# SiLU of convolved channels as one ScalarE function, GpSimd's first-phase work on VectorE, and another order of blocks, banks and priorities in a hybrid decoder layer

## The chip, the cores and the metric

The kernel runs on one core of one Trainium2 chip. A core has five engines that run their own instruction streams in order and wait for one another by semaphores: TensorE (PE, with its weight loads shown apart as PEld), VectorE (DVE), ScalarE (ACT), GpSimd (POOL) and SyncE (SP), which here only issues DMAs. The metric is the device time of one execution in microseconds (us). Before the change the median of three runs is 1030.03 us (1029.24 to 1030.16).

## What is computed

One decoder layer with 16 learned meta tokens ahead of 512 tokens, model width 2048, all float32:

```python
h = rms_norm(concat([meta, x]), norm_w)
(dq, dk, dv, dz, db, da, gq, gk, gv, gz, gl, fq, fk, fv, fz, ff) = split_cols(h @ w_in)
# A: gated DeltaNet, 6 heads x 128
qkv = silu(causal_depthwise_conv(concat([dq, dk, dv], -1), conv_w))
q_dn, k_dn = l2_normalize(q) * 128 ** -0.5, l2_normalize(k)
o_dn = gated_head_norm(gated_delta_rule_chunked(q_dn, k_dn, v_dn, log_a, beta), dz, dn_norm_w)
# B: GLA linear attention, 5 heads (dk 64, dv 128)
o_gla = gated_head_norm(gla_chunked(gq * 64 ** -0.5, gk, gv, log_g), gz, gla_norm_w)
# C: forgetting attention, 5 heads x 128
o_fox = forgetting_attention(fq * 128 ** -0.5, fk, fv, log_f) * silu(fz)
out = rms_norm(x + concat([o_dn, o_gla, o_fox], -1) @ w_out, final_norm_w)
```

`gated_head_norm(o, z, w)` is an RMS norm of each head times `w` and times `silu(z)`. So a SiLU stands in two kinds of place: over the convolved channels dq, dk, dv (18 blocks of 128 channels), and over the gates dz (6 blocks), gz and fz (5 blocks each).

## The kernel before

**The planner.** The kernel is written as many small generators ("chains") that yield operations, events and requests for buffers. A planner, `Weave`, holds an estimate of when each engine is free and when each buffer region is ready (`cost`, `ready`, `emit`), and in `run` always emits the operation with the lowest key: estimated start plus the chain's priority (a lower number goes first), for TensorE plus `SLACK` = 0.25 us. A matmul chain of small ("light") operations is put behind a heavy one when too much light work has come in a row. What it emits is the program order of each engine; so the order is fixed when the kernel is built, and an instruction that is late on the chip holds up all that stands behind it on its engine. All engine calls go through line 251, which is why the profile shows L251 nearly everywhere; tiles, not lines, tell operations apart. `Slots` are pools of buffers: `row` (4 tiles of 128x528), `wide` (9 of 128x1056), `bank` (the 8 PSUM banks), `raw`, `hi`, `lo` (weights as loaded, and split). `Get` waits for a free slot, and where it has `keep`, for more than so many.

**Number format.** A float32 operand is split into a high and a low part (`hp`, `lp` for the pairs, `hb..`, `lb..` for the fill blocks, `ho`, `lo` for the output weights): ScalarE casts the high part, VectorE or GpSimd subtracts it from the operand. A product is three matmuls: high x high, high x low, low x high. `GP = (2,)` sends the subtraction of the second operand of every pair to GpSimd; of the output weights every other one goes there.

**First phase (to 488 us).** Four blocks dz and the gate columns, two more dz (`Z45`), then 18 pairs of 128-column blocks (`PAIRS`, `mm_pair`), each pair as seven half-size products (a Strassen-like scheme; `sums` forms the operands on VectorE, `evac_pair` takes the partial results out of PSUM on ScalarE and VectorE). The pairs alternate between two convolved blocks (dk first, then dv, then dq) and two others (gk, gv, fk, fv). `store` then multiplies the block by the tokens' `rstd` on GpSimd and, for a convolved block, runs `conv`: the first tap on ScalarE, three taps on VectorE, then the SiLU in five steps: a lower bound on GpSimd, Exp, Ln (with bias 1) and Exp on ScalarE, the product on VectorE. `token_rows` transposes the result on TensorE into a bank (`pkdk`, `pkdv`, `pkdq`), takes sums of squares and scaled copies out of it on ScalarE and stores the rows in DRAM. `silu_row` does the same five steps for the gates z (`st..` is its scratch row).

Beside the pairs run `gates` (decay and gate columns, priority 1.0; it sets `e_gate`, for which every `token_rows` waits), `key_scales` (factors of all six key heads at once, as soon as the sums of squares of all six are there; it then starts the next two), `an_blocks` (ten blocks of decay-weighted key products, priority 0.2) and `inverse` (30 steps of two VectorE operations each on tile `ab`, scratch `ot`, which invert 32x32 diagonal blocks).

**Later phases (488 to 1028 us).** The 17 fill blocks (`FILL`: gq, fq, gz, fz in this order) are plain products of 48 matmuls of 512 columns each; they stand in TensorE's order between the mixers' small matmuls. `phase_b` starts when all pairs have left and the inverse is stored: DeltaNet (`dn_group`, `levels`, `core` with its recurrence over blocks, `tail`). `phase_c` runs GLA and the forgetting attention side by side, `phase_d` starts when all fill blocks are done: the output projection (`po`, last column `pz`), the residual, and the final norm (`norm_out`: Ln and Exp on ScalarE for `frs`). Line 345 loads one table set for ScalarE by name:

```python
nc.scalar.preload_act_table_set("natural_log_exp_and_others")
```

The small matmuls that the prediction names: `pm` (DeltaNet's triangular inverse, from `an`), `pks` (the recurrence, from `y`, the result on its way through ScalarE), `pgo` (GLA's output, from `gon`), `pss` (GLA's scores), `pfa`, `pfw` (forgetting attention), `ptl` (the gates' last product, from `scm`).

Of the kernel before, what the change touches and what calls it, by code (L numbers as in the profile page):

```python
# [13 lines left out]
AF = mybir.ActivationFunctionType  # L14
# [59 lines left out]
NBLK = len(COLS) // P  # L74
NROW, NMS, NPB, NWG, NWF, NTS, NOP = 4, 16, 6, 19, 24, 9, 17
GPRI, FPRI = 0.0, 0.0
GP, KX = (2,), 5
AP, KA, BACK, XP = 0.2, 2, 3.0, 0.6
LIGHT, SLACK, DMAL = 0.8, 0.25, 0.8
# [5 lines left out]
class Op:  # L85
    __slots__ = ("eng", "call", "a", "kw", "outs", "ins", "dur", "lat", "dma", "light")

# [55 lines left out]
class Engine:  # L143
# [3 lines left out]
    def __getattr__(self, what):  # L147
        real, key = getattr(self.real, what), self.key

        def make(*a, **kw):  # L150
            op = Op()
            op.eng, op.call, op.a, op.kw = key, real, a, kw
            aps = [x for x in a if isinstance(x, bass.AP)]
            outs = []
            if "out" in kw:
                outs.append(kw["out"])
            elif aps:
                outs.append(aps.pop(0))
# [8 lines left out]
            op.dur, op.lat, op.dma = cost(key, what, n, outs[0], ins)  # L167
            op.light = key == "P" and (n < 64 or ins[0].shape[0] < P or ins[0].free_size() < P)
            return op

        return make
# [38 lines left out]
class Weave:  # L210

    def __init__(self, tc):
        self.tc, self.t, self.last, self.state, self.chains = tc, {}, {}, {}, []
        self.base, self.n, self.light = 0.0, 0, 0.0

# [19 lines left out]
    def emit(self, op):  # L235
        start = max(self.t.get(op.eng, 0.0), self.ready(op))
        if op.eng == "P":
            idle = start - self.t.get("P", 0.0)
            self.light = self.light + idle + op.dur if op.light else max(0.0, self.light + idle - op.dur)
        end = done = start + op.dur  # L240
        self.t[op.eng] = end
        if op.dma:
            self.t["D"] = max(self.t.get("D", 0.0), end + 1.5) + op.dma
            done = self.t["D"] + DMAL
        else:
            done += op.lat
# [4 lines left out]
        i = op.call(*op.a, **op.kw)  # L251
# [7 lines left out]
    def go(self, gen, pri=0.0, name=""):  # L259
        self.n += 1  # L260
        c = [gen, pri, self.n, None, 0.0, name or getattr(gen, "__name__", "")]
        self.chains.append(c)
        self.step(c, None)
# [56 lines left out]
def tile_hybrid_trunk(ctx, tc, xT, xtok, mtok, w_gate, w_in, w_out, consts, lmask, fin_w, out, dbg=None):  # L320
# [19 lines left out]
    tp_s = slots("tp").add(tp, 16, "tp", (P, 2, T))  # L340
    wide_s = slots("wide").add(pa, 9, "pa", (P, 2, T))
    bank_s = slots("bank").add(psp, 8, "k", (P, 512))
# [257 lines left out]

    def key_scales():
        yield tuple(e_nk.values()) + (e_gate,)
        yield A.activation(nbt, gcol[:, :, 0:6], AF.Exp)
        yield A.activation(nbg, gcol[:, :, 6:12], AF.Exp)
        yield A.activation(br, nks, AF.Ln, bias=eps_c)
        yield A.activation(br, br, AF.Exp, scale=-0.5)
        yield V.tensor_tensor(out=nbt, in0=nbt, in1=br, op=ALU.mult)
        yield V.scalar_tensor_tensor(out=nb2, in0=nbt, scalar=-1.0, in1=br, op0=ALU.mult, op1=ALU.mult)
        yield V.tensor_copy(br, nbt)
        yield V.tensor_tensor(out=nbg, in0=nbg, in1=nb2, op=ALU.mult)  # L610
        e_keys.set()
# [7 lines left out]
    e_nk, e_nq, e_keys, e_lq = evs(*range(DN_HEADS)), evs(*range(DN_HEADS)), Ev(), Ev()  # L619
    kds, vps = ([drp.tile([P, NN, P], F32, name=f"{n}{g}") for g in range(2)] for n in ("kds", "vps"))  # L620
# [64 lines left out]
    def token_rows(key, c, u):  # L685
        what, h = key
        g, j = divmod(h, H)
        blocks = [slice(b * P, (b + 1) * P) for b in range(NB)]
        dst, dstm, scale, acc_, ev = {"dk": (kds, kms, dl, nks, e_gate), "dv": (vps, vms, br, None, e_keys),
                                      "dq": (None, None, None, nqs, e_gate)}[what]  # L690
# [78 lines left out]
    def evac_pair(p):  # L769
# [17 lines left out]
        bank_s.give(z)  # L787
        W.go(store(p, 0, u[0]), 0.3, f"store{i}0")
        yield p.done[7]
# [4 lines left out]
        bank_s.give(x)  # L794
        W.go(store(p, 1, u[1]), 0.3, f"store{i}1")
        yield (sp_of(p.keys[0]), sp_of(p.keys[1]))
# [34 lines left out]

    class Block:
# [39 lines left out]
    def operands(seq):  # L872
        yield e_feed
        for it, n in seq:
# [109 lines left out]
    e_A, e_dn, e_fill, e_c, e_gla, e_fox = Ev(), Ev(), Ev(), Ev(), Ev(), Ev()  # L984
    big_s, m_s, pb_s, keep_s = (slots(n) for n in ("big", "m", "pb", "keep"))

    def phase_b():
        yield tuple(p.left for p in pairs) + (e_gate, e_inv)
        early.close()
        W.base = max(W.t.values())  # L990
        kp, bp, mp, pp = pool("kp"), pool("bp", mid), pool("mp", mid), pool("pp", mid)
# [3 lines left out]
        pb_s.add(pp, NPB, "pb", (P, T))  # L995
        for t in range(2):
# [17 lines left out]
    def dn_group(g):  # L1014
# [759 lines left out]
    W.go(loads(), 0.0, "loads")  # L1774
    W.go(key_scales(), 0.1, "scales")
    W.go(mm_main(), 0.25, "mm")
# [67 lines left out]
```

## Time and profile before

| | |
|---|---|
| runs, median (lowest to highest) | 1030.03 us (1029.24 to 1030.16) |
| the profiled execution, its own time | 1029.72 us |
| its span, first to last instruction | 1027.8 us |
| mean granted TensorE clock | 0.985 of full |
| DMA | 144.05 MB, mean 140 GB/s |

The profile shows one execution. For each engine a table of busy time stands first, then 40 equal slices of the span with the busy share of each engine in tenths and the granted clock of TensorE. Groups of instructions are named `out<-in` by the program's tiles with their count, busy time, mean, and the idle time of the engine ahead of them with what ended it. A wait `PE pm <- DMA an<-ans` says that TensorE sat idle ahead of a matmul into `pm` and that the end of that DMA released it. A table of windows gives the same busy times for chosen stretches of the span; restricted to a tile it counts only instructions that read or write it. The slices of TensorE and its clock:

```profile
PE   8999999999999899999998999999999899999996
...
PEclk8999999999999999999998999999999999999998
```

### The profile page before, as it was taken

How to read it: one execution, taken by the hardware profiler on the slowest of the kernel's cores; microseconds unless marked ns; L12 is line 12 of the kernel's file. 1: busy time of each engine (PE TensorE's matmuls, PEld its weight loads, DVE VectorE, ACT ScalarE, POOL GpSimd, SP SyncE). 2: the span in 40 equal slices, each digit the busy share in tenths (PEclk: the TensorE clock that was granted, in tenths of full speed). 3: DMA queues.
4: the chain of work that ended last, by engine and by line, in shares of the span. 5: the costliest groups of instructions: out<-in, count | busy, mean ns of one | idle time of the engine just before them, and what ended most of it. 6: DMA issues, size and time to landing. Idle time of an engine off the chain costs nothing. (4 is left out here: it accounts for less than half of the span.)

```text
span 1027.8 us, 18890 instructions
## 1 busy us (share of the span) xinstructions
PE 983.9 (96%) x7339; PEld 853.3 (83%) x7339; DVE 722.4 (70%) x1178; ACT 535.8 (52%) x1179; POOL 275.3 (27%) x204
## 2 busy tenths in 40 slices
PE   8999999999999899999998999999999899999996
PEld 6889999989999899998776897666767677788885
DVE  6878999778999898888573365857577666633334
ACT  6675555438575675655323574656556543412335
POOL 0022442323344344335101131111131221112451
PEclk8999999999999999999998999999999999999998
DMA  9833222334334354444449526332313444522334
GB/s 325 311 131 124 95 105 74 135 113 153 132 130 152 102 173 146 155 143 117 129 138 318 170 70 217 103 117 84 114 62 104 158 146 148 170 87 82 103 103 163
DMA packets 78060, 144.05 MB, mean 140 GB/s; under 512 B 14461, under 2 KB 38525, under 8 KB 77972
## 3 DMA queue, kind: packets, MB, share of 16 engines
q1 hardware_dynamic: 77972, 142.86, 42.0%
q8 instruction: 57, 0.93, 0.4%
q14 instruction: 31, 0.25, 0.1%
HBM read 119.22 MB, written 23.61 MB: 139 GB/s over the span
## 5 line engine op out<-in xcount | busy, mean ns | idle before, releaser
L251 ACT CAST hp<-a 128x1024 fp32r<-128x1024 f32 x90 | 94.2, 1050 | 60.6 <-PE px L251 35.3
L251 PE MATMUL px<-xh,hp 128*128 128x264 f32 x432 | 125.0, 289 | 0.0
L251 PE MATMUL px<-xh,lp 128*128 128x264 f32 x432 | 123.4, 286 | 1.0 <-DVE lp L251 1.0
L251 PE MATMUL px<-xl,hp 128*128 128x264 f32 x432 | 123.7, 286 | 0.0
L251 DVE SCALAR_TENSOR_TENSOR lp<-a,hp 128x1024 fp32r<-128x1024 f32 x72 | 94.6, 1316 | 20.1 <-ACT hp L251 19.1
L251 POOL TENSOR_TENSOR u<-u,rstd 128x528 f32<-128x528 f32 x36 | 60.1, 1671 | 144.5 <-DVE u L251 109.6
L251 PE MATMUL po<-ho,oh 128*128 128x512 f32 x232 | 93.9, 405 | 1.4 <-ACT oh L251 1.4
L251 PE MATMUL po<-ho,ol 128*128 128x512 f32 x232 | 92.5, 399 | 1.7 <-DVE ol L251 1.7
L251 PE MATMUL po<-lo,oh 128*128 128x512 f32 x232 | 92.1, 397 | 0.0
L251 PE MATMUL px<-tbh,hp 128*128 128x264 f32 x288 | 83.1, 289 | 0.0
L251 PEld LDWEIGHTS px<-xh,lp 128*128 128x128 f32 x432 | 82.0, 190 | 1.2 <-DVE lp L251 1.2
L251 PE MATMUL px<-tbh,lp 128*128 128x264 f32 x288 | 82.3, 286 | 0.5 <-DVE lp L251 0.4
L251 PE MATMUL px<-tah,hp 128*128 128x264 f32 x288 | 82.2, 285 | 0.0
L251 PEld LDWEIGHTS px<-xh,hp 128*128 128x128 f32 x432 | 81.9, 190 | 0.1
L251 PEld LDWEIGHTS px<-xl,hp 128*128 128x128 f32 x432 | 82.0, 190 | 0.0
L251 PE MATMUL px<-tal,hp 128*128 128x264 f32 x288 | 81.9, 284 | 0.0
L251 PE MATMUL px<-tah,lp 128*128 128x264 f32 x288 | 81.8, 284 | 0.0
L251 PE MATMUL px<-tbl,hp 128*128 128x264 f32 x288 | 81.8, 284 | 0.0
L251 ACT CAST ho<-o 128x1024 fp32r<-128x1024 f32 (+1 forms) x35 | 33.9, 976 | 77.2 <-PE po L251 43.6
L251 DVE TENSOR_TENSOR acc<-acc,po 128x512 f32<-128x512 f32 x44 | 29.3, 685 | 53.5 <-PE po L251 53.4
L251 POOL TENSOR_TENSOR lo<-o,ho 128x1024 fp32r<-128x1024 f32 x14 | 33.5, 2396 | 118.5 <-ACT ho L251 100.2
L251 DVE SCALAR_TENSOR_TENSOR cv<-u,cpk,cv 128x525 f32<-128x525 f32 (+2 forms) x54 | 59.5, 1104 | 5.1 <-ACT cv L251 4.2
(375 smaller groups left out, 2748.8 us busy)
## 6 DMA issues: line engine op xcount, KB each, us to landing
a<-in_w_in SPq DMA_DIRECT2D x72, 512.0 KB
o<-in_w_out SPq DMA_DIRECT2D x32, 512.0 KB
rfq<-in_w_in SPq DMA_DIRECT2D x10, 512.0 KB
rgz<-in_w_in SPq DMA_DIRECT2D x10, 512.0 KB
rfz<-in_w_in SPq DMA_DIRECT2D x10, 512.0 KB
fraw<-in_w_in SPq DMA_DIRECT2D x16, 256.0 KB
xt<-in_xtok SPq DMA_DIRECT2D x8, 512.0 KB
acc<-in_xtok SPq DMA_DIRECT2D x16, 256.0 KB
```

Source lines behind the costliest of these rows:

```text
L251: i = op.call(*op.a, **op.kw)
```

## The change

1. **SiLU.** In `conv` the five steps become one ScalarE activation with the function Silu, in place. In `silu_row` the same is done for dz; gz and fz keep the five steps, with the lower bound on VectorE.
2. **GpSimd's work to VectorE.** The product with `rstd` in `store`, the subtractions of operand 2 of the pairs (`GP = ()`), and those of the output weights.
3. **Planner.** It adds 1.3 us where a Silu follows an Exp or Ln on ScalarE or the reverse. A chain can have its own slack for TensorE: 3.0 us for the token rows, 2.0 for the `an` blocks, 1.0 for `levels`. The main matmul chain is served first when slots come free.
4. **Order.** `gates` from priority 1.0 to 0.1, stores from 0.3 to 0.0, `an_blocks` from 0.2 to -0.2. `key_scales` runs once for each group of three heads and starts its own `an` blocks; the scales of the queries and `inverse` (0.05) become chains of their own. The fill blocks go in the order `FORD`.
5. **Buffers.** Two `row` tiles in place of four and ten `wide` in place of nine in the first phase; two more `row` tiles from `phase_b` on; an unused pool is gone.

```diff
-NROW, NMS, NPB, NWG, NWF, NTS, NOP = 4, 16, 6, 19, 24, 9, 17
+NROW, NWIDE, NMS, NWG, NWF, NTS, NOP = 2, 10, 16, 19, 24, 9, 17
-GP, KX = (2,), 5
-AP, KA, BACK, XP = 0.2, 2, 3.0, 0.6
+FORD = 'gq0 fq0 gq1 fq1 fz0 gz0 gz1 fq2 fz1 fq3 fz2 gz2 gz3 fq4 fz3 fz4 gz4'
+STP, IP = 0.0, 0.05
+GP, KX = (), 5
+AP, KA, BACK, XP, GAP = -0.2, 2, 3.0, 0.6, 0.1
...
+            op.fn = {AF.Exp: "e", AF.Ln: "e", AF.Silu: "s"}.get(fn) if key == "A" else None
...
+        if op.fn and op.fn != self.fn:
+            self.fn = op.fn
+            end = done = end + 1.3
...
-            for c in sorted(self.chains, key=lambda c: (c[1], c[2])):
+            for c in sorted(self.chains, key=lambda c: (c[5] != "mm", c[1], c[2])):
...
-                    k = max(c[4] + (SLACK if e == "P" else 0.0), self.t.get(e, 0.0),
+                    k = max(c[4] + (c[6] if e == "P" else 0.0), self.t.get(e, 0.0),
...
     def silu_row(z, key, dst):
+        if key[0] == "dz":
+            yield A.activation(z, z, AF.Silu)
+            yield SP.dma_start(out=dst, in_=z)
+            return
         t = yield Get(row_s, f"st{key[0]}{key[1]}")
-        yield G.tensor_scalar_max(t[:, :S], z, LOW)
+        yield V.tensor_scalar_max(t[:, :S], z, LOW)
...
-    def key_scales():
-        yield tuple(e_nk.values()) + (e_gate,)
...
-        for g in range(2):
-            W.go(an_blocks(g), AP + 0.02 * g, f"an{g}")
-        W.go(inverse(), AP, "inverse")
+    def key_scales(g):
+        c = slice(H * g, H * g + H)
+        yield tuple(e_nk[h] for h in range(c.start, c.stop)) + (e_gate,)
...
+        e_keys[g].set()
+        W.go(an_blocks(g), AP, f"an{g}", 2.0)
...
-        W.go(store(p, 0, u[0]), 0.3, f"store{i}0")
+        W.go(store(p, 0, u[0]), STP, f"store{i}0")
...
     def store(p, n, u):
-        yield G.tensor_tensor(out=u, in0=u, in1=rstd, op=ALU.mult)
+        yield VT(out=u, in0=u, in1=rstd, op=ALU.mult)
...
-            W.go(token_rows(key, c, u), -0.1, f"rows{key[0]}{key[1]}")
+            W.go(token_rows(key, c, u), -0.1, f"rows{key[0]}{key[1]}", 3.0)
...
-        yield G.tensor_scalar_max(t, c, LOW)
-        yield A.activation(t, t, AF.Exp, scale=-1.0)
-        yield A.activation(t, t, AF.Ln, bias=1.0)
-        yield A.activation(t, t, AF.Exp, scale=-1.0)
-        yield VT(out=c, in0=c, in1=t, op=ALU.mult)
+        yield A.activation(c, c, AF.Silu)
...
-    FILL = [Block(("gq", p)) for p in range(2)] + [Block(("fq", h)) for h in range(FOX_HEADS)] \
-        + [Block(("gz", h)) for h in range(GLA_HEADS)] + [Block(("fz", h)) for h in range(FOX_HEADS)]
+    FILL = [Block((k[:2], int(k[2]))) for k in FORD.split()]
...
-                yield from operand(it.src, it.op, it.name, False, True, GT if it.kp % 2 else VT)
+                yield from operand(it.src, it.op, it.name, False, True, VT)
...
+        row_s.add(kp, 4 - NROW, "row_", (P, T))
...
-        W.go(levels(g), -0.2, f"levels{g}")
+        W.go(levels(g), -0.2, f"levels{g}", 1.0)
...
-    W.go(gates(), 1.0, "gates")
+    W.go(gates(), GAP, "gates")
...
-    W.go(key_scales(), 0.1, "scales")
+    for g in range(2):
+        W.go(key_scales(g), 0.1, f"scales{g}")
+    W.go(query_scales(), 0.1, "qscales")
+    W.go(inverse(), IP, "inverse")
```

More of the change, by code (lines that the diff above doesn't have):

```diff
@@ L85 @@
 class Op:
-    __slots__ = ("eng", "call", "a", "kw", "outs", "ins", "dur", "lat", "dma", "light")
+    __slots__ = ("eng", "call", "a", "kw", "outs", "ins", "dur", "lat", "dma", "light", "fn")
 class Ev:
@@ L167, in make @@
             op.dur, op.lat, op.dma = cost(key, what, n, outs[0], ins)
+            fn = next((x for x in a + tuple(kw.values()) if isinstance(x, mybir.ActivationFunctionType)), None)
+            op.fn = {AF.Exp: "e", AF.Ln: "e", AF.Silu: "s"}.get(fn) if key == "A" else None
             op.light = key == "P" and (n < 64 or ins[0].shape[0] < P or ins[0].free_size() < P)
@@ L213, in __init__ @@
         self.tc, self.t, self.last, self.state, self.chains = tc, {}, {}, {}, []
-        self.base, self.n, self.light = 0.0, 0, 0.0
+        self.base, self.n, self.light, self.fn = 0.0, 0, 0.0, "e"
     def begin(self, t, base):
@@ L257, in emit, with go @@
         return start
-    def go(self, gen, pri=0.0, name=""):
+    def go(self, gen, pri=0.0, name="", slack=None):
         self.n += 1
-        c = [gen, pri, self.n, None, 0.0, name or getattr(gen, "__name__", "")]
+        c = [gen, pri, self.n, None, 0.0, name or getattr(gen, "__name__", ""), SLACK if slack is None else slack]
         self.chains.append(c)
@@ L340, in tile_hybrid_trunk @@
     tp_s = slots("tp").add(tp, 16, "tp", (P, 2, T))
-    wide_s = slots("wide").add(pa, 9, "pa", (P, 2, T))
+    wide_s = slots("wide").add(pa, NWIDE, "pa", (P, 2, T))
     bank_s = slots("bank").add(psp, 8, "k", (P, 512))
@@ L599, in gates, with query_scales @@
         e_gate.set()
-    def key_scales():
-        yield tuple(e_nk.values()) + (e_gate,)
[L603 to L611, printed above, removed]
-        for g in range(2):
-            W.go(an_blocks(g), AP + 0.02 * g, f"an{g}")
-        W.go(inverse(), AP, "inverse")
+    def key_scales(g):
+        c = slice(H * g, H * g + H)
+        yield tuple(e_nk[h] for h in range(c.start, c.stop)) + (e_gate,)
+        t, n2, r, ng = (a[:, :, c] for a in (nbt, nb2, br, nbg))
+        yield A.activation(t, gcol[:, :, c], AF.Exp)
+        yield A.activation(ng, gcol[:, :, 6 + c.start : 6 + c.stop], AF.Exp)
+        yield A.activation(r, nks[:, :, c], AF.Ln, bias=eps_c)
+        yield A.activation(r, r, AF.Exp, scale=-0.5)
+        yield V.tensor_tensor(out=t, in0=t, in1=r, op=ALU.mult)
+        yield V.scalar_tensor_tensor(out=n2, in0=t, scalar=-1.0, in1=r, op0=ALU.mult, op1=ALU.mult)
+        yield V.tensor_copy(r, t)
+        yield V.tensor_tensor(out=ng, in0=ng, in1=n2, op=ALU.mult)
+        e_keys[g].set()
+        W.go(an_blocks(g), AP, f"an{g}", 2.0)
+    def query_scales():
         yield tuple(e_nq.values())
@@ L617, in key_scales @@
         e_lq.set()
-    e_nk, e_nq, e_keys, e_lq = evs(*range(DN_HEADS)), evs(*range(DN_HEADS)), Ev(), Ev()
+    e_nk, e_nq, e_keys, e_lq = evs(*range(DN_HEADS)), evs(*range(DN_HEADS)), evs(0, 1), Ev()
     kds, vps = ([drp.tile([P, NN, P], F32, name=f"{n}{g}") for g in range(2)] for n in ("kds", "vps"))
@@ L688, in token_rows @@
         blocks = [slice(b * P, (b + 1) * P) for b in range(NB)]
-        dst, dstm, scale, acc_, ev = {"dk": (kds, kms, dl, nks, e_gate), "dv": (vps, vms, br, None, e_keys),
+        dst, dstm, scale, acc_, ev = {"dk": (kds, kms, dl, nks, e_gate), "dv": (vps, vms, br, None, e_keys[g]),
                                       "dq": (None, None, None, nqs, e_gate)}[what]
@@ L794, in evac_pair @@
         bank_s.give(x)
-        W.go(store(p, 1, u[1]), 0.3, f"store{i}1")
+        W.go(store(p, 1, u[1]), STP, f"store{i}1")
         yield (sp_of(p.keys[0]), sp_of(p.keys[1]))
@@ L984, in tile_hybrid_trunk @@
     e_A, e_dn, e_fill, e_c, e_gla, e_fox = Ev(), Ev(), Ev(), Ev(), Ev(), Ev()
-    big_s, m_s, pb_s, keep_s = (slots(n) for n in ("big", "m", "pb", "keep"))
+    big_s, m_s, keep_s = (slots(n) for n in ("big", "m", "keep"))
     def phase_b():
@@ L990, in phase_b @@
         W.base = max(W.t.values())
-        kp, bp, mp, pp = pool("kp"), pool("bp", mid), pool("mp", mid), pool("pp", mid)
+        kp, bp, mp = pool("kp"), pool("bp", mid), pool("mp", mid)
         keep_s.add(kp, 2, "kp", (P, NN, P))
@@ L994, in phase_b @@
         m_s.add(mp, NMS, "m", (P, H, P))
-        pb_s.add(pp, NPB, "pb", (P, T))
+        row_s.add(kp, 4 - NROW, "row_", (P, T))
         for t in range(2):
```

## The prediction

> **What bounds the kernel now.** The page first, then the table of windows, cut where the TensorE (PE) changes its work: 87.4 to 488.5 us holds the 18 projection pairs (the first phase), 488.5 to 1018.9 the fill blocks, the three mixers and the output projection. Columns: busy us and instructions of PE, its weight loads, VectorE (DVE), ScalarE (ACT), GpSimd (POOL), then granted PE clock, DMA share, GB/s.
>
> ```profile
> PE 983.9 (96%) x7339; PEld 853.3 (83%) x7339; DVE 722.4 (70%) x1178; ACT 535.8 (52%) x1179; POOL 275.3 (27%) x204
> ```
>
> ```profile
> 87.40:488.50 401.10, 387.32 (x3148) 382.49 (x3147) 352.22 (x355) 234.70 (x465) 150.56 (x82) 1.00 0.39 128
> 488.50:1018.90 530.40, 513.38 (x3810) 402.54 (x3809) 301.01 (x712) 240.19 (x617) 111.73 (x101) 0.99 0.40 131
> 204.00:222.00 18.00, 15.86 (x117) 15.36 (x116) 13.35 (x19) 5.87 (x8) 5.58 (x3) 0.91 0.27 94
> 542.00:556.00 14.00, 10.42 (x170) 7.78 (x171) 4.20 (x10) 4.87 (x9) 0.88 (x2) 0.76 1.04 360
> 817.40:845.00 27.60, 23.25 (x94) 18.41 (x94) 19.40 (x29) 14.33 (x27) 8.66 (x7) 0.88 0.43 141
> ```
>
> PE is busy in 387.32 of 401.10 us and in 513.38 of 530.40. The change neither adds nor removes a matmul, so it can only take PE's idle time and the clock lost behind it: 13.8 + 17.0 us idle, and in the last three windows busy time at less than full clock, 15.86 x 0.09 = 1.4, 10.42 x 0.24 = 2.5 and 23.25 x 0.12 = 2.8 us. Next the table of waits for PE alone, by phase (us in total, times, longest):
>
> ```profile
> PE pkdv L251 <- DVE cv L251: 5.4, 4, 1.8
> PE pkdq L251 <- DVE cv L251: 2.8, 2, 2.2
> PE pkdk L251 <- DVE cv L251: 2.2, 1, 2.2
> PE px L251 <- DVE lp L251: 1.3, 2, 1.0
> PE ptl L251 <- DVE scm L251: 1.2, 1, 1.2
> ```
>
> ```profile
> PE pm L251 <- DMA an<-ans: 3.6, 1, 3.6
> PE po L251 <- DVE ol L251: 1.7, 1, 1.7
> PE pfa L251 <- DVE fp L251: 1.7, 2, 1.4
> PE pss L251 <- DVE qx L251: 1.7, 1, 1.7
> PE po L251 <- ACT oh L251: 1.4, 1, 1.4
> PE pfw L251 <- DVE ml L251: 1.3, 2, 1.2
> PE pkdq L251 <- DVE cv L251: 1.1, 1, 1.1
> ```
>
> The greatest cause is one chain: the token rows (`pkdk`, `pkdv`, `pkdq`) are transposed on PE straight after the SiLU of a convolved channel, and PE reaches them before it is done: 5.4 + 2.8 + 2.2 + 1.1 = 11.5 us. The rest is small and scattered.
>
> **The change, part by part.**
>
> *SiLU and GpSimd's work.* By tile (ns min/median/max):
>
> ```profile
> L251 POOL TENSOR_TENSOR u<-u,rstd x36: 1314/1482/2292, 103.0 to 505.0; 128x528 f32<-128x528 f32 x36
> L251 POOL TENSOR_SCALAR u<-cv x18: 1525/2165/2707, 110.4 to 485.4; 128x528 f32<-128x528 f32 x18
> ```
>
> ```profile
> L251 ACT ACTIVATE u<-u x54: 626/644/649, 114.0 to 491.7; 128x528 f32<-128x528 f32 x54
> ```
>
> ```profile
> L251 DVE SCALAR_TENSOR_TENSOR cv<-u,cpk,cv x54: 752/768/2966, 105.7 to 484.2; 128x525 f32<-128x525 f32 x18, 128x526 f32<-128x526 f32 x18, 128x527 f32<-128x527 f32 x18
> L251 DVE SCALAR_TENSOR_TENSOR cv<-cv,u x18: 691/698/2896, 118.9 to 493.3; 128x528 f32<-128x528 f32 x18
> ```
>
> ```profile
> L251 DVE SCALAR_TENSOR_TENSOR lp<-a,hp x72: 1206/1222/2285, 77.7 to 491.9; 128x1024 fp32r<-128x1024 f32 x72
> ```
>
> A convolved channel loses GpSimd's maximum (2.165), two of three activations (2 x 0.644) and VectorE's product (0.698): the chain ahead of the transposes is 4.2 us shorter. The table set that line 345 loads is named for Exp and Ln; whether a Silu needs another no row shows, and I assume that it does. The one load in the trace:
>
> ```profile
> 0.73 1.28 ACT L345 ACT_TABLE_LOAD   x1 [0.73 <-PEq L1836]
> ```
>
> So 2.9 us are left even where each Silu pays a load, against a longest wait of 2.2; and the planner now sets the transposes 3.0 us after it thinks them ready, and costs the load at 1.3. I take 10.5 of the 11.5 us, between 0 and 11.5. How long a Silu takes no row shows; between 0.6 (`u<-u`) and three of those, I take one. The six gate blocks z of the DeltaNet get the same cut; PE waits for none of them. Two `row` tiles for four hold them back more; the ends are 0 and 3 us (the row of the longest wait but one, 2.2, rounded up), and I take 0, since PE has its pairs to do meanwhile and takes banks first.
>
> VectorE takes over 36 products with `rstd`, 18 operand subtractions (`lp` of operand 2) and, later, 14 `lo` and ten maxima. It is at 352.22 of 401.10 us already, so this decides. But the maxima of the rows above are far over their minima, on VectorE, where GpSimd works beside it. The same window for the instructions on `cv`, then on `a`, shows the total:
>
> ```profile
> 87.40:488.50 401.10, 13.66 (x80) 8.50 (x80) 77.17 (x71) 19.40 (x42) 36.80 (x18) 1.00 0.39 128
> ```
>
> ```profile
> 87.40:488.50 401.10, 195.75 (x141) 91.09 (x87) 44.50 (x17) 1.00 0.39 128
> ```
>
> The first has 54 steps and 17 products: at their minima 54 x 0.752 + 17 x 0.691 = 52.4, so 24.8 of 77.17 us are stretch. The second (columns DVE, ACT, POOL) has 141 instructions of one size: 141 x 1.206 = 170.0, stretch 25.7. GpSimd's 150.56 us go but for the masks of the `an` blocks, under 9 us,
>
> ```profile
> L251 POOL TENSOR_SCALAR_AFFINE_SELECT an<-an 128x384 f32<-128x384 f32 x8 | 7.5, 935 | 21.9 <-DMA an<-gd 21.4 <-PE px L251 0.5
> ```
>
> and I let the stretch go with them: 352.2 - 50.5 - 11.7 (products) + 35 x 0.691 + 17 x 1.206 = 334.7. The inverse, which moves into this phase, adds:
>
> ```profile
> 488.50:545.00 56.50, 20.92 (x60) 1.00 0.48 142
> ```
>
> That makes 356 of 401: no new bound, and `lp` half as long as GpSimd's. Cost 0; if the stretch stayed, 414 (below).
>
> *Order of gates, key scales, inverse.* With priority 0.1 for 1.0 the gates run earlier, when their inputs are there; the waits for `scm` and `lp` (1.2, and 1.0 of the 1.3) and their clock (1.4) stand in the window 204 to 222. I take 2.5 of 3.6; a wait may come back elsewhere, so the ends are -1 and 3.6. Key scales by group and priority -0.2 start the ten `an` blocks and the inverse earlier, their DMAs on SP's queue with them (five issues for each `an` block, ten for the inverse), ahead of weight loads; the raw weights have buffers, and VectorE's, not GpSimd's, results are what SP then waits for. The phase after it starts with its inputs in DRAM, and one of PE's longest waits, `pm` on `an<-ans` (3.6, and 2.5 of clock), has more fill blocks to stand behind: I take 4, between 0 and 6.1. Four more short activations and four more short products of the split scales are 2 us on engines with room.
>
> *Order of the fill blocks, banks to matmuls first, stores earlier.* The handover at 817 (3.1 of waits, 2.8 of clock) keeps its chain (cast, subtraction, matmul); only its subtraction loses GpSimd beside it: 1, between -3 and 5.9. Of `pfa`, `pss`, `pfw` (4.7) I take 1, between -4 and 4.7: a new order makes waits of its own.
>
> **Gain: 10.5 + 2.5 + 4 + 1 + 1 = 19 us.**
>
> *What the Silu does to Exp and Ln.* The kernel names one table set for both, by hand, once, at the start; the trace has that one load. The diff names it nowhere again. If a load after a Silu is placed for the function that is next, Exp and Ln may not share a set from then on, and every Ln among Exps costs two loads. Of Lns after the last Silu there are, by row and by code:
>
> ```profile
> L251 ACT ACTIVATE f<-f,eps_c x8: 281/297/313, 587.0 to 621.8; 128x3 f32<-128x3 f32 x8
> ```
>
> ```profile
> L251 ACT ACTIVATE gso<-gso,eps_c x5: 297/297/298, 689.4 to 789.8; 128x4 f32<-128x4 f32 x5
> ```
>
> ```profile
> L251 ACT ACTIVATE frs<-frs,eps_c x4: 294/294/295, 1008.7 to 1020.7; 128x1 f32<-128x1 f32 x4
> ```
>
> and ten in the SiLU of the other gate blocks, three in the GLA gates: 30, so up to 60 loads x 1.28 = 77 us, which the planner doesn't know of. ScalarE is busy in 240.19 of 530.40 us, 45%; a load in its idle time costs nothing, so some 27 delay something. How much of that PE has in hand differs:
>
> ```profile
> 586.63 0.48 ACT L251 COPY y<-pks 128x384 f32<-128x384 f32 x1 [0.56 <-PE pks L251]
> ```
>
> ```profile
> 587.16 0.94 PE L251 MATMUL pks<-y,kd 128*128 128x128 f32 x6
> ```
>
> ```profile
> 689.98 1.14 ACT L251 ACTIVATE gon<-pgo,gso 128x128 f32<-128x128 f32 x4
> ```
>
> ```profile
> 692.59 0.27 PE L251 MATMUL pgo<-ident,gon 128*128 128x128 f32 x1
> ```
>
> 0.05 us in the recurrence (587.11 to 587.16), 1.47 in the GLA output. A load that PE feels costs from 1.23 to 0, the middle 0.62; half of the 27 stand ahead of something buffered (weight casts, gate blocks): 27 x 0.5 x 0.62 = 8.4 us, between 0 and 27 x 1.23 = 33.
>
> ```profile
> L251 DVE TENSOR_REDUCE frs<-fss x4: 157/158/158, 1008.5 to 1020.5; 128x1 f32<-128x4 f32 x3, 128x1 f32<-128x5 f32 x1
> ```
>
> The last Ln and Exp lie on the path to the end, and only this reduction of 0.16 us covers a part of the first load: 2 x 1.28 - 0.16 = 2.4. In the first phase 24 Silus can bring 48 loads, less than ScalarE's 166 idle us; the copies out of PSUM that PE needs have eight steps of three matmuls to be late, 24 x 401/3148 = 3.1 us: I take 1, between 0 and 5.
>
> The Trainium skill ("ScalarE: Activation LUTs", What ACT_TABLE_LOAD costs) gives 1283 ns for the load, which the row has, and about 1380 ns of drain at every switch, which no row here can show, since the one load has nothing ahead of it. By the page a switch would be 2.66 us, and the cost above some 25 + 5 for 8.4 + 2.4.
>
> **Sum.** The profiled execution took 1029.72 us (median of the runs 1030.03): 1029.7 - 19 + 8.4 + 2.4 + 1 = **1022.5 us**.
>
> **Rivals.**
> - *Exp and Ln go on sharing a set.* For it: nothing in their code changes. Against: the set had to be named by hand. No loads after the last Silu: 1029.7 - 19 + 1 = 1012.
> - *The loads bind (slower).* Same mechanism, in the recurrence and in GLA and fox, where chains of ScalarE and PE alternate with 0.05 us in hand. If each of the 27 is paid, 33 + 2.4 + 1 - 19 = +17: 1047. It turns the sign once those 27 cost PE over (19 - 3.4)/27 = 0.58 us each; I hold 0.31.
> - *A switch empties the engine.* At two loads' length (2.57), 27 x 0.5 x (2.57 - 0.76) + 4.8 + 1 - 19 = +11: 1041. This is the page's drain.
> - *VectorE becomes the bound.* If the stretch is not GpSimd's, all goes at the mean, 77.17/71 = 1.09 and 195.75/141 = 1.39: 352.2 - 17 x 1.09 + 35 x 0.691 x 77.17/52.4 + 17 x 1.39 + 20.9 = 414 > 401. The phase grows by 13 and its 13 of gain go: 1029.7 + 13 - 6 + 11 = 1048. Against: minima of 0.69 and 1.21 in the same rows.
> - *The waits only move*, as a hand-set order does: 1030.
>
> **How the numbers follow.** Forecast 0.42, shared set 0.12, loads bind 0.24, drain 0.07, VectorE 0.06, waits move 0.09. Faster by over 0.2% (about what a measurement of this kernel can tell from no change) 0.54, same 0.09, slower 0.37. The forecast's own range is 1012 to 1029; with the other cases 1006 to 1046, which leaves out half of the 1047s and a little below.
>
> **What would show it.** Right: waits of `pkd*` on `cv` under 2 us in all; VectorE near 355 us in the first phase, `lp` at 1.22; loads before Ln and Exp after 490 us, some 60, and PE's waits on ScalarE up by about 8 us. Wrong: no loads there (1012), or PE idle in 570 to 625 us grown by over 8 us (1047), or VectorE's instructions on `a` still at 1.39 on average.

## The result, and the profile after

The changed kernel takes 1055.41 us (median of 4 runs, 1054.77 to 1056.65) against 1030.1 of the kernel before: ratio 1.0244, 95% interval 1.0225 to 1.0263. It is slower by 25 us; the prediction said 1022.5, with 1006 to 1046 as its range.

The page of the changed kernel: the TensorE row, the slices of TensorE and its clock, and the shares of the chain that ended last by line.

```profile
PE 991.3 (94%) x7339; PEld 861.3 (82%) x7339; DVE 703.3 (67%) x1236; ACT 617.3 (59%) x1219; POOL 72.2 (7%) x102
...
PE   8999999999999999999899799988989979999994
...
PEclk8999999999999999999999899999999989999997
...
PE px L258 33%; PE po L258 15%; ACT L258 6%; PE pz L258 5%; PE pbfz L258 4%; PE pbfq L258 3%; PE pbgz L258 2%; PE pbdz L258 2%; PE pg L258 1%; PE pfa L258 1%; PE pgo L258 1%; PE pbgq L258 1%; PE pfw L258 1%; ACT on L258 1%; ACT gon L258 1%
```

Two things differ from before. The first half is full: the nines run from slice 2 to slice 19. From slice 20 on eights and sevens stand among them. And the chain that ended last has a line "ACT L258" without a tile, 6% of the span: these are the table loads. Their row among the groups of ScalarE (where one stood before):

```profile
L258 ACT ACT_TABLE_LOAD x84 | 107.8, 1283 | 2.9 <-DVE cv L258 1.3
```

Counted along the timeline, 30 loads (with the one at the start) lie in the first phase, 15 in DeltaNet's recurrence, 32 in GLA and the forgetting attention, 8 in the final norm: 55 behind the pairs.

The table of windows, cut at the same events in both kernels (pairs; recurrence up to GLA's first matmul; GLA and forgetting attention; last matmul to the end). The fill blocks stand elsewhere in the new order, so the second and third stretch hold other numbers of matmuls before and after (419 and 562, 2221 and 2065). First the one before, whose pairs stand in 87.6 to 504.5, then the one after; columns as in the prediction.

```profile
87.60:504.50 416.90, 402.06 (x3225) 394.84 (x3225) 358.40 (x368) 241.89 (x481) 151.46 (x83) 1.00 0.39 128
572.00:629.60 57.60, 56.52 (x419) 49.95 (x417) 30.33 (x91) 36.11 (x143) 16.18 (x26) 1.00 0.38 114
629.60:902.00 272.40, 261.74 (x2221) 194.96 (x2221) 181.09 (x462) 142.06 (x364) 47.84 (x45) 0.99 0.38 127
1019.50:1027.80 8.30, 0.00 (x1) 0.00 (x0) 1.73 (x4) 2.34 (x6) 0.00 (x0) 0.63 0.72 235
```

```profile
89.50:485.20 395.70, 395.12 (x3218) 391.95 (x3217) 336.64 (x414) 252.13 (x470) 10.23 (x14) 1.00 0.42 135
...
533.20:613.20 80.00, 70.79 (x562) 61.14 (x555) 33.85 (x102) 62.74 (x171) 15.54 (x23) 0.91 0.37 113
613.20:877.00 263.80, 235.13 (x2065) 172.06 (x2065) 166.64 (x457) 173.03 (x385) 24.98 (x34) 0.95 0.33 109
...
1037.00:1052.70 15.70, 0.00 (x0) 0.00 (x0) 3.28 (x9) 10.31 (x18) 0.00 (x0) 0.60 0.57 187
```

In the pairs TensorE's idle time falls from 14.84 to 0.58 us, and nearly the same matmuls take 21 us less. Then it turns: in the recurrence 9.2 us idle (1.1 before) and a granted clock of 0.91, in GLA and the forgetting attention 28.7 us idle (10.7 before) and 0.95, and from the last matmul to the end 15.7 us for 8.3. TensorE's waits, the longest causes:

```profile
PE pgo L258 <- ACT gon L258: 6.9, 3, 3.6
PE po L258 <- ACT on L258: 5.9, 4, 3.5
PE pfa L258 <- DVE fsm L258: 4.7, 3, 2.3
PE pfa L258 <- DVE fp L258: 4.1, 4, 2.8
```

None of the waits for `cv` is left; ScalarE's results lead now. One of these waits in the timeline, ScalarE first, then TensorE (start, duration, in brackets the idle time ahead and who ended it):

```profile
696.65 0.25 ACT L258 ACTIVATION_READ_ACCUMULATOR gon<-pgo 128x1 f32 x1
696.92 1.28 ACT L258 ACT_TABLE_LOAD   x1
698.21 0.30 ACT L258 ACTIVATE gso<-gso,eps_c 128x4 f32<-128x4 f32 x1
698.53 1.28 ACT L258 ACT_TABLE_LOAD   x1
699.82 0.20 ACT L258 ACTIVATE gso<-gso 128x4 f32<-128x4 f32 x1
700.06 1.14 ACT L258 ACTIVATE gon<-pgo,gso 128x128 f32<-128x128 f32 x4
```

```profile
697.06 0.39 PE L258 MATMUL pbfq<-xl,hbfq 128*128 128x512 f32 x1
697.29 0.39 PE L258 MATMUL pbfq<-xh,lbfq 128*128 128x512 f32 x1
701.26 0.66 PE L258 MATMUL pgo<-ident,gon 128*128 128x128 f32 x4 [3.58 <-ACT gon L258]
701.67 0.48 PE L258 MATMUL pbfq<-xh,hbfq 128*128 128x512 f32 x1
...
702.26 0.63 PE L258 MATMUL pbfq<-xh,lbfq 128*128 128x512 f32 x1
...
703.34 0.63 PE L258 MATMUL pbfq<-xl,hbfq 128*128 128x512 f32 x1
703.76 0.63 PE L258 MATMUL pbfq<-xh,lbfq 128*128 128x512 f32 x1
```

A Ln and an Exp of 0.5 us have become 3.1 us with their two loads. TensorE sits for 3.58 us in front of `pgo`, though the matmuls of a fill block (`pbfq`), whose operands are there, stand right behind: its order is fixed. And when it goes on, the same matmul that took 0.39 us takes 0.63 soon after.

### The profile page after: what moved, and what is told of

Read it like the earlier page. It is cut to its first block, busy times and chain, and to the rows that moved or that the text cites. A ratio compares the mean times of both kernels' runs of the same rounds, so it can differ in the third digit from the quotient of the medians.

```text
span 1052.7 us, 18846 instructions
## 1 busy us (share of the span) xinstructions
PE 991.3 (94%) x7339; PEld 861.3 (82%) x7339; DVE 703.3 (67%) x1236; ACT 617.3 (59%) x1219; POOL 72.2 (7%) x102
## 4 chain that ended last, share of the span: by engine, by line
PE 73%; ACT 14%; DVE 6%; DMA 3%; issue 2%; SPq 1%; ACTq 0%; POOL 0%; DVEq 0%; POOLq 0%
PE px L258 33%; PE po L258 15%; ACT L258 6%; PE pz L258 5%; PE pbfz L258 4%; PE pbfq L258 3%; PE pbgz L258 2%; PE pbdz L258 2%; PE pg L258 1%; PE pfa L258 1%; PE pgo L258 1%; PE pbgq L258 1%; PE pfw L258 1%; ACT on L258 1%; ACT gon L258 1%
## 5 line engine op out<-in xcount | busy, mean ns | idle before, releaser
L258 DVE SCALAR_TENSOR_TENSOR lp<-a,hp 128x1024 fp32r<-128x1024 f32 x90 | 110.1, 1223 | 31.9 <-ACT hp L258 31.5
L258 ACT CAST hp<-a 128x1024 fp32r<-128x1024 f32 x90 | 94.5, 1049 | 60.9 <-PE px L258 37.4
L258 PE MATMUL px<-xh,hp 128*128 128x264 f32 x432 | 124.1, 287 | 0.1
L258 PE MATMUL px<-xl,hp 128*128 128x264 f32 x432 | 122.9, 284 | 0.0
L258 PE MATMUL px<-xh,lp 128*128 128x264 f32 x432 | 122.6, 284 | 0.0
L258 ACT ACT_TABLE_LOAD x84 | 107.8, 1283 | 2.9 <-DVE cv L258 1.3
L258 PE MATMUL po<-ho,oh 128*128 128x512 f32 x232 | 92.6, 399 | 0.9 <-ACT oh L258 0.9
L258 ACT CAST ho<-o 128x1024 fp32r<-128x1024 f32 (+1 forms) x35 | 33.9, 977 | 100.8 <-PE po L258 58.8
L258 PE MATMUL po<-ho,ol 128*128 128x512 f32 x232 | 92.2, 397 | 0.8 <-DVE ol L258 0.8
L258 PE MATMUL po<-lo,oh 128*128 128x512 f32 x232 | 91.9, 396 | 0.0
L258 DVE SCALAR_TENSOR_TENSOR lo<-o,ho 128x1024 fp32r<-128x1024 f32 (+1 forms) x35 | 40.9, 1176 | 71.4 <-ACT ho L258 71.2
L258 PE MATMUL px<-tbh,hp 128*128 128x264 f32 x288 | 82.8, 288 | 0.0
L258 PE MATMUL px<-tah,hp 128*128 128x264 f32 x288 | 82.5, 286 | 0.0
L258 PE MATMUL px<-tbl,hp 128*128 128x264 f32 x288 | 81.9, 284 | 0.0
L258 PE MATMUL px<-tah,lp 128*128 128x264 f32 x288 | 81.9, 284 | 0.0
L258 PE MATMUL px<-tal,hp 128*128 128x264 f32 x288 | 81.8, 284 | 0.0
L258 PE MATMUL px<-tbh,lp 128*128 128x264 f32 x288 | 81.8, 284 | 0.0
L258 PEld LDWEIGHTS px<-xh,hp 128*128 128x128 f32 x432 | 81.3, 188 | 0.5 <-ACT u L258 0.3
L258 PEld LDWEIGHTS px<-xl,hp 128*128 128x128 f32 x432 | 81.3, 188 | 0.0
L258 PEld LDWEIGHTS px<-xh,lp 128*128 128x128 f32 x432 | 81.2, 188 | 0.0
L258 PEld LDWEIGHTS px<-tbh,hp 128*128 128x128 f32 x288 | 54.3, 188 | 0.2
L258 PEld LDWEIGHTS px<-tbh,lp 128*128 128x128 f32 x288 | 54.2, 188 | 0.0
```

## The experiments

The time of the kernel before, measured beside each set, had medians of 1030.5 to 1032.0; ratios are to it. Theory A: the loads behind the pairs cost the whole loss among the mixers and in the tail. Its rival B: the new order and VectorE's added work lose it.

**1. Name the shared set once more, after the last Silu.**

```diff
     def query_scales():
         yield tuple(e_nq.values())
+        W.named_set("natural_log_exp_and_others")
         yield A.activation(nqs, nqs, AF.Ln, bias=eps_c)
```

(`named_set` is a new method of the planner: it issues `preload_act_table_set` and keeps it in ScalarE's program order.)

> The changed kernel, with the shared set of Exp and Ln named a second time, straight after the last Silu and ahead of the queries' Ln: one load there, and none of the 55 that the changed kernel has after 488 us. Everything else, the order of all instructions too, stays. Theory A (loads bind): from the windows the changed kernel has 32 us more PE idle and 14 us more clock loss than the one before from the end of the pairs on, and all of it is due to those loads, so 1055.4 - 46 = 1009, with 1005 to 1016 as the bounds; the tail from the last matmul to the end is 8.3 us again. Theory B (the new order of the fill blocks and VectorE's added work lose the time among the mixers, the loads mostly hide): 1045 to 1053. Theory C (half and half): near 1030.

Measured 996.33 us, ratio 0.9663 (0.9637 to 0.969). Apart from the loads the instructions of all five engines stand in the order of the changed kernel, so the difference is that of 55 loads: 1055.4 - 996.3 = 59 us, 1.07 us each. B falls. A holds in kind, but the time is 9 us below its lowest bound of 1005: the loads cost more than the waits and the clock that A had counted. The table of windows of this kernel, same stages:

```profile
89.70:484.80 395.10, 394.96 (x3218) 391.88 (x3218) 336.70 (x413) 252.09 (x469) 10.20 (x14) 1.00 0.42 135
...
532.20:597.00 64.80, 64.55 (x562) 56.65 (x556) 34.33 (x102) 43.07 (x156) 14.97 (x22) 1.00 0.43 134
597.00:825.70 228.70, 223.92 (x2065) 165.63 (x2065) 166.16 (x457) 132.71 (x353) 24.67 (x34) 0.99 0.38 128
...
985.70:994.00 8.30, 0.01 (x1) 0.00 (x0) 1.73 (x4) 2.34 (x6) 0.00 (x0) 0.69 0.72 236
```

With the same 562 and 2065 matmuls the recurrence is 15.2 us shorter (15 loads), GLA and the forgetting attention 35.1 (32 loads), the tail 7.4 (8 loads). That is 0.9 to 1.1 us for each load in all three. Of the first two, 50.3 us, 32.9 are TensorE's idle time (9.21 + 28.67 against 0.25 + 4.78) and 17.4 are its own busy time, which grew as its clock fell (70.79 + 235.13 against 64.55 + 223.92).

**2. Name it after every Silu**, where the planner sees the change from Silu to Exp or Ln:

```diff
         if op.fn and op.fn != self.fn:
             self.fn = op.fn
             end = done = end + 1.3
+            if op.fn == "e":
+                self.named_set("natural_log_exp_and_others")
```

> As the run before it, but the shared set is named each time that an Exp or Ln follows a Silu, in the first phase too: about 11 pairs of loads there become 11 single returns. Theory A: PE is idle for 0.6 us in the whole first phase, so nothing is to be had there: within 1.5 us of the run that names the set once. Theory D (loads in the first phase delay the next phase by way of key scales, decay blocks or ScalarE's copies): 2 to 6 us below that run.

995.85 us, ratio 0.9651 (0.9626 to 0.9677): no different from naming it once. But only five loads are gone by it (25 in all for 30), so it says little of the others of the first phase. What the windows show is that TensorE is idle in the pairs for 0.58 us in the changed kernel, and for 0.14 us in run 1, with 24 loads there in both. This kernel is the base of runs 6 and 10 to 14.

**3. Loads alone.** The kernel before, and after its queries' Ln the set of Exp alone is named; no Silu, no other order.

```diff
         yield A.activation(nqs, nqs, AF.Ln, bias=eps_c)
+        W.named_set("exp_and_others")
```

> The kernel before, untouched but for one load: the set of Exp alone is named after the queries' Ln, so that from then on every Ln among Exps brings two loads, with no Silu, no new order and GpSimd's work where it was. Theory A: 30 Lns, some 55 loads, and the price that the changed kernel shows: 1030 + 40 to 46 = 1070 to 1076. Theory B: at the price of my prediction, 11 us, or less: 1035 to 1041.

1092.57 us, ratio 1.0596 (1.0573 to 1.062), above the 1070 to 1076 that theory A expected. Its row of loads, and the longest of its waits, which is that of the changed kernel:

```profile
L251 ACT ACT_TABLE_LOAD x56 | 71.8, 1283 | 1.0
```

```profile
PE pgo L251 <- ACT gon L251: 8.6, 3, 3.9
```

56 loads cost 61.7 us, 1.10 each, in the order of the kernel before and with no Silu at all. The price belongs to the loads, and what brings them is that the set in use no longer serves both functions.

**4. The tail alone.** The shared set is named ahead of the first Ln of the final norm.

> The changed kernel, the shared set named only ahead of the first Ln of the final norm: the 8 loads of the tail become one. Theory A: the tail's 15.7 us from the last matmul to the end go back to the 8.3 of before, so 1055.4 - 7.4 = 1048. My prediction's own price for the tail, 2.4: 1053. The rest of the loss stays in both.

1048.81 us, ratio 1.0176 (1.0154 to 1.0198): 6.6 us for the tail's loads, not 2.4. ScalarE's timeline of the changed kernel at the third of the four rows shows why:

```profile
1037.79 1.28 ACT L258 ACT_TABLE_LOAD   x1
1039.09 0.29 ACT L258 ACTIVATE frs<-frs,eps_c 128x1 f32<-128x1 f32 x1
1039.40 1.28 ACT L258 ACT_TABLE_LOAD   x1
1040.69 0.20 ACT L258 ACTIVATE frs<-frs 128x1 f32<-128x1 f32 x1
1040.93 1.33 ACT L258 ACTIVATE acc<-acc,frs 128x512 f32<-128x512 f32 x2
1042.16 0.40 ACT L258 ACTIVATE sqf<-acc 128x256 f32<-128x256 f32 x1
```

TensorE is done at 1037.0, but ScalarE is still at the third row's loads, and the squares of the last row start at 1042.16. The rows queue: the loads of the rows ahead are paid too.

**5. Tell the planner.** The changed kernel, no set named; the planner charges 1.3 us for a change from Exp to Ln and back too.

```diff
-            op.fn = {AF.Exp: "e", AF.Ln: "e", AF.Silu: "s"}.get(fn) if key == "A" else None
+            op.fn = {AF.Exp: "e", AF.Ln: "l", AF.Silu: "s"}.get(fn) if key == "A" else None
...
-        if op.fn and op.fn != self.fn:
+        if op.fn and op.fn not in self.fn:
```

(`self.fn` starts as "el", the shared set.)

> The changed kernel, no set named again; only the planner is told that an Exp after a Ln and a Ln after an Exp cost 1.3 us each once a Silu has been there, so it places TensorE's order around them. Theory A1 (the loads are paid because the order was fixed without them; TensorE has fill blocks enough to stand in the gaps): half or more of the 51 us that the 47 loads cost ahead of the tail comes back: 1015 to 1035. Theory A2 (the chains of ScalarE and TensorE are serial there, no order hides them): 1045 to 1055.

1019.03 us, ratio 0.9884 (0.9845 to 0.9923). Its loads:

```profile
L258 ACT ACT_TABLE_LOAD x90 | 115.5, 1283 | 4.2 <-DVE cv L258 2.6
```

With 59 loads behind the pairs for 55, 36 of the 59 us come back by the order alone (A1). Most of the price is not the load itself but a fixed order that was set without it; 23 us stay. A new order can gain or lose several us by itself (runs 9 and 15), so the 36 is rough.

The other runs ask what the gain beside the loads consists of: 1030 to 996 is 34 us, where the prediction summed 19.

**6. GpSimd's work given back** (product with `rstd`, every second operand, every other output weight, lower bounds), on the kernel of run 2.

```diff
-GP, KX = (), 5
+GP, KX = (2,), 5
...
-        yield VT(out=u, in0=u, in1=rstd, op=ALU.mult)
+        yield G.tensor_tensor(out=u, in0=u, in1=rstd, op=ALU.mult)
...
-                yield from operand(it.src, it.op, it.name, False, True, VT)
+                yield from operand(it.src, it.op, it.name, False, True, GT if it.kp % 2 else VT)
```

> The kernel that names the shared set after each Silu (995.85), with GpSimd's element-wise work given back: the product with rstd, the subtraction of every second operand, of every other output weight, and the lower bounds of gz and fz. Theory E1 (GpSimd beside VectorE stretches both, and its operand is late): VectorE's instructions on cv and a are again far over their minima, TensorE idle in the first phase 5 to 15 us more: 1001 to 1012. Theory E2 (TensorE has enough in hand): 994 to 998.

1014.32 us, ratio 0.9847 (0.9812 to 0.9881): 18.5 us, more than E1. Windows of the pairs, the longest waits for the pairs' operands, and a row of VectorE (ns, min, median and max):

```profile
90.36:502.53 412.17, 401.27 (x3218) 394.73 (x3217) 347.67 (x391) 242.16 (x463) 112.05 (x64) 1.00 0.40 130
```

```profile
PE px L260 <- DVE lp L260: 4.6, 7, 1.1
PE px L260 <- POOL lp L260: 2.8, 1, 2.8
```

```profile
L260 DVE SCALAR_TENSOR_TENSOR cv<-u,cpk,cv x54: 750/767/2873, 112.5 to 484.1; 128x525 f32<-128x525 f32 x18, 128x526 f32<-128x526 f32 x18, 128x527 f32<-128x527 f32 x18
```

The pairs take 412.17 us again, of which 10.9 idle, where the kernel of run 1 has 395.10 and 0.1, with the same 3218 matmuls. The long maximum is back with GpSimd (2873 ns; 903 in run 1). So VectorE, which takes the work over, serves TensorE better without GpSimd beside it, and is even busy for less: 336.7 us against 347.67. Idle time makes up 10.8 of the 17.1 us; the same matmuls are also busy for 6.3 us longer at a granted clock of 1.00, and no run shows why.

**7. The five steps given back** in `conv` and for dz (lower bound on VectorE), so no Silu at all.

> The changed kernel with the SiLU of the convolved channels and of dz in the five steps of before (lower bound on VectorE): no Silu, so one load in all. Against the kernel that names the set (996): theory F1 (the Silu itself is worth the waits of the token rows): the chain ahead of the transposes is 3 to 4 us longer, VectorE has some 28 us more in the first phase (about 365 of 395): 1000 to 1010. Theory F2 (the 3.0 us of slack and the order have done it already): 994 to 999.

1023.17 us, ratio 0.9935 (0.9898 to 0.9972), 27 us above run 2, beyond F1. Two single waits make up much of it:

```profile
PE px L258 <- ACT tah L258: 8.7, 1, 8.7
PE pkd L258 <- DVE gst L258: 8.1, 1, 8.1
```

Neither is on a convolved channel. How much of the 27 us is the SiLU's length and how much the order that came out is left open.

**8. The Silu alone**, on the kernel before, the shared set named after each, the planner charging 1.3 us per change.

> The kernel before with the Silu alone, for the convolved channels and dz; the shared set is named after each, and the planner charges 1.3 us for each change. Nothing else moves: GpSimd's work, priorities, order of blocks. Theory G1 (the 11.5 us of waits for cv are the length of the SiLU): 8 to 11 us off: 1019 to 1022. Theory G2 (the planner puts the transposes where it thinks them ready, so the wait moves along): 1027 to 1031.

1033.92 us, ratio 1.0039 (1.0021 to 1.0057): no gain, rather 0.4% slower, and 3 us above G2. The waits:

```profile
PE pfa L258 <- DVE fp L258: 10.7, 2, 10.3
PE pkdq L258 <- ACT cv L258: 3.8, 3, 2.3
...
PE pkdk L258 <- ACT cv L258: 2.2, 1, 2.2
PE pkdv L258 <- ACT cv L258: 1.7, 1, 1.7
```

7.7 us of the 11.4 on `cv` are still there, with a shorter chain: the planner puts the transposes where it now thinks them ready, and the wait moves along. Another wait of 10.3 us, far away, is new and hides what the Silu may gain: how much that is without it this run does not tell.

**9. The slack alone**, on the kernel before: 3.0 us for the token rows.

```diff
-            W.go(token_rows(key, c, u), -0.1, f"rows{key[0]}{key[1]}")
+            W.go(token_rows(key, c, u), -0.1, f"rows{key[0]}{key[1]}", 3.0)
```

> The kernel before with one edit: the token rows' slack for TensorE is 3.0 us in place of 0.25. Theory H1: the 11.4 us of waits on cv go, with nothing else changed: 1017 to 1022. Theory H2 (TensorE then finds the banks or the next operands late): 1027 to 1033.

1011.87 us, ratio 0.9804 (0.9771 to 0.9837), 5 us below H1. One number of the planner takes all waits for `cv` away; VectorE's operands are late then (6.5 us of waits of `px` on `lp`).

**10, 11. The slack back to 0.25 us, and the order of the fill blocks back**, each on the kernel of run 2.

> The kernel that names the shared set after each Silu (995.85), with the token rows' slack back from 3.0 to 0.25 us. Theory H1 (the slack, not the shorter SiLU, took the waits of the token rows away): some 8 us of waits of pkdk, pkdv and pkdq on cv come back, as in the run with the Silu alone (3.8 + 2.2 + 1.7): 1002 to 1006. Theory H2 (the Silu with GpSimd gone is never late): 994 to 998.

> The kernel that names the shared set after each Silu (995.85), with the fill blocks in the order of before (gq, fq, gz, fz). Theory J1 (the new order of the fill blocks is what gains among the mixers, where 14 us went beside the loads): 1002 to 1010. Theory J2 (the order is worth what my prediction gave it, about 1 us): 994 to 999.

999.23 us (ratio 0.9689, 0.9661 to 0.9717) and 997.71 us (0.9679, 0.9653 to 0.9705). Against run 2 (0.9651, 0.9626 to 0.9677) both intervals overlap: with the Silu and without GpSimd the slack is worth some 3 us and the order of the blocks some 2, and neither is told from nothing. With the old slack one wait of 2.0 us for `cv` is back, not the 8 us of H1.

**12. Silu for gz and fz too**, in place of their five steps.

> The kernel that names the shared set after each Silu (995.85), with Silu for gz and fz too; the planner knows the loads. Each of ten blocks loses two activations of 0.64 and two operations of VectorE and gets up to two loads of 1.28 us. Theory K1 (a shorter chain, loads that the order is built around): 989 to 996. Theory K2 (up to 20 more loads among the mixers cost near 0.5 us each, as in the run whose planner knew of them): 1000 to 1008.

1003.43 us, ratio 0.9734 (0.971 to 0.9758): 7.6 us slower than run 2, though ten blocks lose four operations each, as K2 expected. There are 18 more loads (43 for 25); that they are the cause was not tested apart.

**13 to 16. How far the order alone carries.** Slack 2.5 and 3.5 on the kernel of run 2, slack 2.5 on the kernel before, and Silu with slack 3.0 on the kernel before.

> The kernel that names the shared set after each Silu (995.85), with 2.5 in place of 3.0 us of slack for the token rows. No wait is near that limit, so only the order moves. Theory O1 (the order alone carries little): 993 to 999. Theory O2 (one order differs from the next by as much as the single edits did, by a stall of 8 to 10 us here or there): anything from 990 to 1012.

> The same with 3.5 us. Theory O1: 993 to 999. Theory O2: anything from 990 to 1012.

> The kernel before with 2.5 us of slack for the token rows, where 3.0 gave 1011.87. Theory O1: 1009 to 1015. Theory O2: the gain of 19 us is partly the order's: 1016 to 1024, about the 11 us that the waits account for.

> The kernel before with both the Silu (shared set named after each) and 3.0 us of slack. Theory P1 (both take away the same waits, and the Silu adds no more): 1009 to 1015, as with the slack alone. Theory P2 (the shorter chain and less work on ScalarE add to it): 1000 to 1007.

995.3 and 995.72 us on the kernel of run 2: robust. 1018.59 us (ratio 0.9863, 0.9821 to 0.9905) on the kernel before: 7 us from 1011.87, of which one wait for `cv` is 0.4, so nearly all of it is the order's doing. 1016.57 us with the Silu as well (0.9837, 0.979 to 0.9885), between these two and just above P1: on the kernel before the Silu adds nothing to the slack that can be told from the order. What it adds in the changed kernel stays open, as run 7 leaves it.

## Why the prediction was wrong

**The step that failed is the price of the loads**, "27 x 0.5 x 0.62 = 8.4 us", with the tail's 2.4. The mechanism stood there: no shared set after a Silu, about 60 loads (55 came), 1.283 us each. The price of all 55 is 59 us. The sign that I gave for it came as well: in the recurrence TensorE is idle for 9.2 us where it was 1.1. Three factors of that term were wrong, and the tail's with them.

- *The 27.* I took ScalarE's idle share, 55%, as a place where loads hide. But its idle time there is waiting for other links of such chains: in run 1, from 532 to 826 us, its longest waits are for `fsm` (13.7 us) and `gd` (11.3) from VectorE. A load ahead of a Ln and one ahead of its Exp lengthen the chain that they stand in whatever the share; all 47 together cost 50.3 us, 1.07 each.
- *The half "ahead of something buffered".* A fill block covers a late result only if it stands ahead of it in TensorE's order. The wait of 3.58 us at `pgo` has its fill block behind it. Run 5 bears on this: with the loads known to the planner 36 of 59 us return.
- *The 0.62.* It had no share for the clock. Of the 1.07 us a load, 0.70 is TensorE's idle time (32.9 us) and 0.37 its own busy time, which grew by 17.4 us in these stages.
- *The tail's 2.4.* I charged the last row alone. The loads of the rows ahead are paid too: 7.4 us by the windows, 6.6 by run 4.

So the rival "the loads bind" holds, in the place that I gave it; its 1.23 us per load is near the 1.07 that was measured, but it charged only 27. With all 55 at 1.07 in place of 8.4 + 2.4 + 1, my sum would have been 1029.7 - 19 + 59 = 1070; that the kernel came out at 1055 is due to a gain that I also had too small. That the rival's 1047 lies near is luck: too few loads and too small a gain offset each other.

**The gain, 34 us for 19.** Of the 34 some 20 are there by the end of the pairs (504.5 us before, 484.8 in run 1), and 14 come from there to the last matmul (515.0 and 500.9 us). By its terms:

- *Waits of the token rows, 10.5.* They are gone. The cause that I led with, the shorter chain, leaves 7.7 of the 11.4 us when it comes alone (run 8); I had the slack as a second reason, and it takes all of them away (run 9). With the Silu and without GpSimd the old slack leaves 2.0 (run 10).
- *VectorE takes GpSimd's work at no cost.* Right: the stretch went. The rows of VectorE on `cv` and `lp` after, min, median and max in ns, against maxima of 2966 and 2285 before:

```profile
L258 DVE SCALAR_TENSOR_TENSOR cv<-u,cpk,cv x54: 746/760/903, 109.7 to 467.1; 128x525 f32<-128x525 f32 x18, 128x526 f32<-128x526 f32 x18, 128x527 f32<-128x527 f32 x18
```

```profile
L258 DVE SCALAR_TENSOR_TENSOR lp<-a,hp x90: 1206/1224/1268, 77.9 to 471.8; 128x1024 fp32r<-128x1024 f32 x90
```

  VectorE is busy for 337 us in the pairs, 355 were forecast, so it is not the bound. But I booked this only as "no cost". It is a gain, 18.5 us in run 6, and the greatest omission on that side: the wait rows of before put 1.3 us on `lp`, and I took that for all that GpSimd was worth.
- *The gates, 2.5.* The waits for `scm` and `lp` are gone, but not by the priority alone: with the new priority and GpSimd's work given back (run 6) the wait for `scm` is 1.2 us again, as before, and those for `lp` are 7.4 us.
- *`pm`, 4.* The wait went from 3.6 to 2.8 us: about 1.
- *Order of the blocks, 1, and the handover, 1.* Right within what run 11 can tell.
- *Loads of the first phase, 1.* Of TensorE's idle time in the pairs, no more than 0.58 us.

Of the 14 us behind the pairs run 6 gives GpSimd some 2 (503.1 us for 500.9), and run 11 gives the blocks' order at most a few. The priorities, the other slacks and the buffers were not tried apart, so most of these 14 us have no cause shown.

**The other rivals.** The shared set does not stay by itself; it does once it is named again, and then the time is 996. A drain at each switch: in the rows above the load starts 0.02 us after the instruction ahead of it has ended and the next starts 0.01 us after the load. The Trainium skill ("ScalarE: Activation LUTs", What ACT_TABLE_LOAD costs) gives 1283 ns for the load, which the row of loads confirms, and about 1380 ns of drain, which no row here shows. At its 2.66 us for each switch 55 loads would take 146 us, an estimate, where all of their cost is 59. VectorE as the bound, and waits that only move, fall for the first phase; run 8 shows that the second holds for the Silu taken alone.

## What to carry to other kernels

Where a function from another table set comes in, look for what the old set was shared by: here one line that names the set again turns 2.4% slower into 3.4% faster (1055 to 996 us). Where the order of instructions is fixed ahead of time, a delay that the order doesn't know of can be paid nearly in full, however idle its engine looks: here the loads in the pairs cost next to nothing, and those in chains between ScalarE and TensorE about 1.07 us of their 1.28. Price it by the chain it stands in, and add the clock. And a short wait on a row does not tell what an engine is worth that slows another: compare minima with maxima of the same operation, and book what comes free.

## What was not expected of the hardware

A wait of TensorE costs more than its length. The 512-column matmuls, which started 0.23 us apart ahead of the wait of 3.58 us (697.06, 697.29), start 0.42 apart 2 us behind it (703.34, 703.76). Shorter waits are followed by the same. These are the windows of 3.5 us that start where a wait of 2.26 us and one of 2.13 us end:

```profile
637.40:640.90 3.50, 3.44 (x12) 2.93 (x13) 3.18 (x7) 2.54 (x5) 3.50 (x5) 0.53 0.07 25
770.50:774.00 3.50, 3.46 (x11) 2.97 (x12) 2.67 (x3) 2.31 (x10) 0.00 (x0) 0.52 0.61 184
```

TensorE is busy in nearly all of both, at a granted clock of 0.53 and 0.52; behind a wait of 1.99 us, from 757.1 us on, it is 1.00. In the recurrence 9.2 us of idle time stand beside a granted clock of 0.91, which lengthened the busy time by 6.2 us. And loads of 1.28 us among instructions of 0.2 us left no other trace on ScalarE: its busy time rose by 70.1 us for 55 loads (617.3 against 547.2), 70.6 by their rows.
